# A hybrid decoder layer on one core: the recurrence's last unit, the attention's first operands and the sample's recurrence change places

## The chip, the cores and the metric

The kernel runs on one core of one Trainium2 chip. The time is that of one launch on the device, in microseconds (us); before the change it is 3038.96 us, the median of three runs (3030.53 to 3044.77). Everything lives in one program: matmuls on TensorE (PE), elementwise work on VectorE (DVE), ScalarE (ACT) and GpSimd (POOL), and nearly all transfers are issued by SyncE (SP).

## What is computed

One layer of a decoder, in float32, for a prompt of 2048 tokens and for 8 sample requests of 4 tokens each (32 rows), which share the weights:

```
a = rmsnorm(h); [qa|fa|ia|ga|qb|kb|vb] = a @ w_in          # 1024 -> 4*512 + 3*512
h = h + concat(HGRN2(qa,fa,ia,ga), DilatedAttn(qb,kb,vb)) @ w_o
h = h + ConvFFN(rmsnorm(h))                                # 1024 -> 2816 -> 1024
h = h + sigmoid(rmsnorm(h) @ w_ple_gate) * (p @ w_ple_proj)
y = rmsnorm(h)
```

HGRN2 is a gated linear recurrence with 4 heads of width 128, `S_t = diag(f_t) S_{t-1} + k_t v_t^T`, `o_t = S_t^T q_t`, which the kernel evaluates by chunks of 128 tokens. The attention has 8 heads of width 64 and three dilated windows (1, 4 and 16 apart). For the sample, both start from a given state: a matrix per request and head, and 2048 cached keys and values per request. Outputs are the two `y`, the states, the keys and values, and the shifted caches.

## The kernel before

A product of two float32 matrices is made of three fast ones: each operand is split into a rounded part and a remainder (`wh`/`wl`, `xh`/`xl`), and three of the four products are summed (`mm3`, lines 142 to 144; lines 344 to 346 when the tokens stand in the rows).

**Projections** (`in_phase`, once per block of tokens: 0 to 1023, then 1024 to 2079). Feature groups (qa, fa, ga) go to `ha_d` in DRAM, token groups to `va_d` (the recurrence's values), `v_d`, `qT_d` and `kT_d`. The second block's order is i, qa, fa, ga, a marker `H`, then v, q, k.

**The prompt's recurrence** (`hgrn_unit`): 8 units, each of 512 tokens and two heads, unit 0 first. A unit is a chain over DVE, PE, ACT and POOL in about ten steps; the state `S` of each head passes from unit to unit. The generator `hgrn(lo, hi)` makes units `lo` to `hi - 1`. Units 0 to 6 are woven into the second block's projections: 0 to 3 at two steps per group ahead of the marker, 4 to 6 at one step per group behind it. Unit 7 is woven into the attention, with the spare PSUM pool `pps` (tiles `s`).

**Attention** (`attn_phase`, stepped as `main`). For each pair of heads p and each 512 tokens c, `stage` loads rotated queries and keys from DRAM, and `stack` splits them (POOL lines 148, 654, 659; DVE 655; ACT 658). Then come units of work over 128 queries: scores on PE (762, 763), mask, add and minimum in one DVE instruction (767, it needs the constant `mask`, line 671), exponential on ACT (768), transposes (775), a copy (777) and the weighted sum (787). A head in one unit is one exponential, so the 256 exponentials count the stage's progress. Results of two dilations are merged through small DRAM round trips. The first stage's first chunk uses the tiles `ssq` and `rb` of the projections as staging.

**Beside the attention** runs the generator `others()`: unit 7 of the recurrence, then the sample's attention (`attn_sample`, 32 loads `skt` of 1 MB each from the caches, matmuls 887 and 923), then the sample's recurrence (`hgrn_sample`, lines 551 to 629: loads of the state, DVE 616, PE 610 and 613). It advances one step on every second turn of `main`.

**Trunk** (`trunk`): output projection, feed-forward (Strassen products, lines 1207 to 1360, weights prepared on ACT 180 and DVE 181, sums into `h` at DVE 1248) and embedding. `embed_prep` splits the input of the embedding (ACT 1390, DVE 1392) and sums squares for its norm (`sum_sq`: ACT 1004, add at line 1005, on POOL by `eng=G`).

**What sets the order.** The program is written as generators that are stepped against each other; a list scheduler then fixes the order of each engine's instructions when the program is built. `first(gen, n)` gives a generator's steps a priority of 1000 instructions ahead (`AHEAD`). On the chip each engine takes its own list strictly in order and waits on semaphores. SyncE's list is one queue too: a load behind a store waits until the store's data is computed. Each of its transfers also waits until the transfer eight places ahead of it has landed, since it takes that one's semaphore. Pools of SBUF are opened and closed as stacks from the left or the right; a tile in a reused place waits for the last reader of what lay there.

Of the kernel before, what the change touches and what calls it, by code (L numbers as in the profile page):

```python
# [11 lines left out]
F32 = mybir.dt.float32  # L12
# [35 lines left out]
def hymba_step_kernel(ctx: ExitStack, tc: tile.TileContext, I: dict, O: dict):  # L48
# [387 lines left out]
    def hgrn_unit(u, heads, S, ld, wk, sp, plv, po, pms, msk):  # L436

        u0 = 512 * u
        st = {}
# [80 lines left out]
        for i, h in enumerate(heads):  # L520
# [5 lines left out]
            for c in range(4):  # L526
# [3 lines left out]
                s = sp.tile([128, 128], F32, name=f"S{h}")  # L530
# [21 lines left out]
    def hgrn_sample(hp, pps):  # L552
# [50 lines left out]
        for bb in range(8):  # L603
            s0 = hp.tile([128, 4, 128], F32, name="hs0", bufs=2)
# [30 lines left out]
    def attn_phase(spare, rest):  # L635

        def stage(p, c, tiles=()):

            out = []
            for i, src in enumerate((qT_d, kT_d)):  # L640
                t = tiles[i] if tiles else dp.tile([128, 2, 512], F32, name="stage", bufs=4)
# [19 lines left out]
        first = stage(0, 0, [t[:, :1024].rearrange("p (h t) -> p h t", h=2) for t in spare])  # L661
        yield
        dp, rp, wk, sm, pS, pA, pT = rest()
# [5 lines left out]
        kL = rp.tile([128, 2, 4, 512], F32R, name="kL")  # L669
        mask = wk.tile([128, 768], F32, name="mask", bufs=1)  # L670
        SP.dma_start(mask, I["amask"])
        stack(0, *first)
        yield
# [127 lines left out]
        todo, staged = {}, []  # L801
# [9 lines left out]
        for p in range(4):  # L811
            for c in range(4):
# [6 lines left out]
                elif c:  # L819
                    at(x - 12, lambda c=c: staged.append(stage(0, c)))  # L820
                    at(x - 6, lambda c=c: stack(c, *staged.pop(0)))
# [119 lines left out]
    def trunk(cst, rp, ev, sm, tw, hp, sh, wp, dw, pmm, pdn):  # L941
# [435 lines left out]
        def embed_prep(b, s):  # L1377
# [8 lines left out]
            for m in range(NK):  # L1386
# [4 lines left out]
                sum_sq(m, hm, s.ssq, T, eng=G)  # L1391
# [128 lines left out]
    pms = args[-1]  # L1520
    plv, po = pool("h_plv", 3, space=PSUM), pool("h_po", 1, space=PSUM)
# [33 lines left out]
    for h in range(4):  # L1555
        s = sp.tile([128, 128], F32, name=f"S{h}")
# [4 lines left out]
    main, rest = None, []  # L1561
    for x in in_phase(1, *args, plv, po):
        if x == "hgrn":
            first(side, 1000)
            side = hgrn(4, 7, *psum)
            main = attn_phase(args[0][2:], lambda: rest)
            step(main, 1)
        else:
            first(side, 2 if main else 1)
    first(side, 1000)  # L1570
    in_st.close()
    pool = pools(attn_st)
    pps = pool("s_ps", 1, space=PSUM)
    rest += (pool("a_d", 2), pool("a_r", 1), pool("a_w", 3), pool("a_s", 3),
             pool("a_pS", 2, space=PSUM), pool("a_pA", 2, space=PSUM), pool("a_pT", 2, space=PSUM))
    step(main, 1)

    def others():
        yield from hgrn(7, 8, from_pool(pps, "s1", "s2"), from_pool(pps, "s1"), from_pool(pps, "s2"))
        for h in range(4):  # L1580
            SP.dma_start(O["ps"][h], S[h])
        hgrn_st.close()
        with ExitStack() as st:
            pool = pools(st)
            yield from attn_sample(pool("s_c", 1), pool("s_k", 3), pool("s_w", 1), pps)
# [169 lines left out]
```

## Time and profile before

| what | value |
|---|---|
| median of 3 runs | 3038.96 us (3030.53 to 3044.77) |
| the profiled execution: own time | 3035.49 us |
| its span, first to last instruction | 3033.7 us |
| mean granted TensorE clock | 0.987 |
| projections (first matmul to the last of line 346) | 0 to 829 us |
| attention, until the output projection's first matmul | 829 to 1225 us |
| trunk | 1225 to 3034 us |

Groups of instructions are shown as line, engine, operation, tile written and read, shape and count; then busy time, the mean of one in ns, and the idle time of the engine ahead of them with what ended it. A row of stretches gives, for each engine, the busy time and the count in the stretch, then the granted clock of PE (1.00 is full speed), the share of the 16 DMA engines that was busy, and GB/s.

### The profile page before, as it was taken

The page shows a single profiled execution, that of the slowest core. Times are in us where ns is not written, and L with a number is a line of the kernel's source. Part 1 is how long each engine was busy: PE and PEld are TensorE (multiplying, and loading weights), DVE is VectorE, ACT ScalarE, POOL GpSimd, SP SyncE. Part 2 cuts the span into 40 slices and gives each one's busy share as a digit, 9 for nine tenths or more (in the row PEclk, how much of TensorE's full clock was granted, in tenths as well). Part 3 has the DMA queues.
Part 4 walks back from the last instruction along what each step waited for, and adds up shares of the span by engine and source line. Part 5 has one row for each costly group of instructions (what it writes and reads, how often), then busy time and mean ns, then how long its engine had stood idle before and what let it go on. Part 6 is the DMA issues. An engine that isn't in the chain of part 4 may idle for free.

```text
span 3033.7 us, 52104 instructions
## 1 busy us (share of the span) xinstructions
PE 2927.9 (97%) x18639; PEld 2716.8 (90%) x18639; DVE 2252.7 (74%) x4847; ACT 1310.1 (43%) x2824; POOL 736.8 (24%) x758
## 2 busy tenths in 40 slices
PE   8999999999988899999999999999999999999998
PEld 8988799988776557999999999999999999998987
DVE  7657766876588777658988888766679777777777
ACT  5332422222166665434544444544444544444443
POOL 1343222212244443102443431000001000002331
PEclk9999999999989999999999999999999999999999
DMA  5899533342338996766666568677778777787773
GB/s 184 312 338 324 175 101 102 110 130 94 111 101 230 269 271 185 250 230 220 229 213 195 190 197 297 230 249 253 242 239 312 249 236 243 242 275 280 263 253 130
DMA packets 328579, 664.08 MB, mean 219 GB/s; under 512 B 46400, under 2 KB 114112, under 8 KB 326528
## 3 DMA queue, kind: packets, MB, share of 16 engines
q1 hardware_dynamic: 291472, 472.65, 47.8%
q0 software_dynamic: 33264, 121.13, 12.5%
q10 hardware_dynamic: 3584, 66.98, 6.0%
q8 instruction: 147, 2.41, 0.3%
q14 instruction: 112, 0.92, 0.1%
HBM read 513.69 MB, written 213.92 MB: 240 GB/s over the span
## 4 chain that ended last, share of the span: by engine, by line
PE 53%; DVE 6%; issue 2%; DMA 1%; ACT 1%; POOL 0%; SPq 0%; DVEq 0%; POOLq 0%; ACTq 0%
PE mm L142 17%; PE mm L144 17%; PE mm L143 17%; DVE h L1248 1%; DVE w L181 1%; PE acc L787 1%; PE PT L775 1%; DVE w L1392 1%; DMA w<-h_d 0%; DMA out_yT_dram<-w 0%; PE mm L129 0%; PE S L762 0%; DVE h L1098 0%; PE s L923 0%; PE s L613 0%
## 5 line engine op out<-in xcount | busy, mean ns | idle before, releaser
L143 PE MATMUL mm<-w 128*128 128x348 f32 (+3 forms) x3636 | 1166.2, 321 | 3.4 <-DVE w L1392 3.2
L142 PE MATMUL mm<-w 128*128 128x348 f32 (+3 forms) x3508 | 1110.6, 323 | 21.1 <-ACT s L1190 7.7
L144 PE MATMUL mm<-w 128*128 128x348 f32 (+3 forms) x3508 | 1117.3, 321 | 2.0 <-DVE w L181 2.0
L143 PEld LDWEIGHTS mm<-w 128*128 128x128 f32 x3636 | 684.2, 188 | 6.7 <-DVE w L1392 4.5
L142 PEld LDWEIGHTS mm<-w 128*128 128x128 f32 x3508 | 656.5, 188 | 30.4 <-ACT s L1190 9.9
L144 PEld LDWEIGHTS mm<-w 128*128 128x128 f32 x3508 | 658.9, 188 | 3.2 <-DVE w L181 2.4
L181 DVE TENSOR_TENSOR w<-raw,w 128x512 fp32r<-128x512 f32 x586 | 434.1, 746 | 182.2 <-ACT w L180 175.7
L180 ACT CAST w<-raw 128x512 fp32r<-128x512 f32 x586 | 360.5, 621 | 413.3 <-PE mm L144 295.8
L1232 POOL DMA_DIRECT2D w<-wd_d x231 | 123.9, 537 | 894.8 <-PE mm L144 788.9
L1248 DVE TENSOR_TENSOR h<-h,mm 128x348 f32<-128x348 f32 (+1 forms) x504 | 247.4, 507 | 44.4 <-PE mm L144 42.8
L768 ACT ACTIVATE P<-P,st 128x256 f32<-128x256 f32 (+3 forms) x256 | 134.3, 526 | 72.2 <-DVE st L767 66.5
L1190 ACT COPY s<-mm 128x348 f32<-128x348 f32 (+1 forms) x198 | 87.9, 444 | 154.4 <-PE mm L144 154.2
L344 PE MATMUL mm<-wh,xh 128*128 128x512 f32 x352 | 141.8, 406 | 0.0
L345 PE MATMUL mm<-wl,xh 128*128 128x512 f32 x352 | 140.5, 399 | 0.3 <-DVE wl L267 0.3
L346 PE MATMUL mm<-wh,xl 128*128 128x512 f32 x352 | 140.6, 400 | 0.0
L144 PE MATMUL mm<-xh,wl 128*128 128x384 f32 (+2 forms) x384 | 125.1, 330 | 5.0 <-DVE wl L267 5.0
L142 PE MATMUL mm<-xh,wh 128*128 128x384 f32 (+2 forms) x384 | 124.5, 329 | 5.6 <-ACT xh L242 5.3
L143 PE MATMUL mm<-xl,wh 128*128 128x384 f32 (+2 forms) x384 | 125.5, 328 | 1.7 <-DVE xl L243 1.7
L767 DVE CUSTOM_DVE_ANT_0 P<-S,mask 128x256 f32<-128x256 f32 (+3 forms) x256 | 106.1, 447 | 26.9 <-PE S L763 19.3
L1005 POOL TENSOR_TENSOR w<-w 128x696 f32<-128x696 f32 (+2 forms) x42 | 75.6, 1808 | 171.1 <-ACT w L1004 162.1
L787 PE MATMUL acc<-pt,v 128*64 128x128 f32 x1136 | 102.9, 300 | 12.8 <-DVE pt L777 11.4
L267 DVE TENSOR_TENSOR wl<-wraw,wh 128x512 fp32r<-128x512 f32 x104 | 89.1, 878 | 28.3 <-POOL wh L148 23.1
(356 smaller groups left out, 5252.5 us busy)
## 6 DMA issues: line engine op xcount, KB each, us to landing
w<-wd_d POOLq DMA_DIRECT2D x231, 512.0 KB, 5.4
wd_d<-dw SPq DMA_DIRECT2D x77, 512.0 KB
out_sk_dram<-in_cache_k_dram ACTq DMA_DIRECT2D x56, 584.0 KB
out_sv_dram<-in_cache_v_dram ACTq DMA_DIRECT2D x56, 584.0 KB
raw<-in_w_gate_dram SPq DMA_DIRECT2D x110, 256.0 KB
raw<-in_w_up_dram SPq DMA_DIRECT2D x110, 256.0 KB
wraw<-in_w_in_dram SPq DMA_DIRECT2D x104, 256.0 KB
raw<-w_gate_d SPq DMA_DIRECT2D x88, 256.0 KB
```

The costliest lines, as they stand in the source:

```text
L142: PE.matmul(ps, lhsT=wh, rhs=xh, start=first, stop=False, skip_group_check=read)
L143: PE.matmul(ps, lhsT=wh, rhs=xl, start=False, stop=False, skip_group_check=read)
L144: PE.matmul(ps, lhsT=wl, rhs=xh, start=False, stop=last, skip_group_check=read)
L180: A.copy(w[:, 0], raw)
L181: V.tensor_sub(w[:, 1], raw, f32(w[:, 0]))
L344: PE.matmul(ps, lhsT=xh[k][:, js], rhs=wh, start=k == 0, stop=False)
L345: PE.matmul(ps, lhsT=xh[k][:, js], rhs=wl, start=False, stop=False)
L346: PE.matmul(ps, lhsT=xl[k][:, js], rhs=wh, start=False, stop=k == NK - 1)
L768: A.activation(pe, pe, AF.Exp, bias=mn, scale=-1.0, accum_out=st[:, bl.r, hh, 0:1])
L787: PE.matmul(acc[hs, bl.r], lhsT=vals[bl.p, bl.di, c][:, r, hs], rhs=bl.pt[hh][:, i], start=i == 0, stop=i == bl.nk - 1, tile_position=(0, ...
L1232: G.dma_start(t, wd_d[p][n - 1])
L1248: V.tensor_add(o, o, acc[m][:, :H])
```

## The change

All eight units of the prompt's recurrence are now stepped in the second block's projections: behind the marker `hgrn(4, 8)` is stepped three steps per group. When it is done, its state is stored and its SBUF (right side) and PSUM (`more_st`) are given back; the attention's operand pool (`a_r`: qS, q4, kH, kL) and staging pool (`a_d`) open there, and the stages and stacks of the first two chunks are stepped while the projections go on. `others()` now holds the sample's recurrence first, then the sample's attention, with all their pools open at once, and advances on two turns of five. The states `S` have 5 buffers, the sample's state loads 4 instead of 2. In `embed_prep` the sum of squares is added on VectorE instead of GpSimd.

```diff
-                s = sp.tile([128, 128], F32, name=f"S{h}")
+                s = sp.tile([128, 128], F32, name=f"S{h}", bufs=5)
...
-            s0 = hp.tile([128, 4, 128], F32, name="hs0", bufs=2)
+            s0 = hp.tile([128, 4, 128], F32, name="hs0", bufs=4)
...
-        def stage(p, c, tiles=()):
+        rp, dp = early
+        spare = [t[:, :1024].rearrange("p (h t) -> p h t", h=2) for t in spare]
+
+        def stage(p, c):
...
-                t = tiles[i] if tiles else dp.tile([128, 2, 512], F32, name="stage", bufs=4)
+                t = dp.tile([128, 2, 512], F32, name="stage") if c % 2 else spare[i]
...
-        first = stage(0, 0, [t[:, :1024].rearrange("p (h t) -> p h t", h=2) for t in spare])
-        yield
-        dp, rp, wk, sm, pS, pA, pT = rest()
...
+        staged = [stage(0, 0), stage(0, 1)]
+        for c in range(2):
+            stack(c, *staged.pop(0))
+            yield
+        wk, sm, pS, pA, pT = rest
         mask = wk.tile([128, 768], F32, name="mask", bufs=1)
         SP.dma_start(mask, I["amask"])
-        stack(0, *first)
-        yield
...
-                elif c:
+                elif c > 1:
...
-                sum_sq(m, hm, s.ssq, T, eng=G)
+                sum_sq(m, hm, s.ssq, T)
...
     for x in in_phase(1, *args, plv, po):
         if x == "hgrn":
             first(side, 1000)
-            side = hgrn(4, 7, *psum)
-            main = attn_phase(args[0][2:], lambda: rest)
-            step(main, 1)
-        else:
-            first(side, 2 if main else 1)
-    first(side, 1000)
+            side, late = hgrn(4, 8, *psum), True
+        elif main:
+            step(main, 1 if begun < 2 else 0)
+            begun += 1
+        elif not first(side, 3 if late else 2) and late:
+            for h in range(4):
+                SP.dma_start(O["ps"][h], S[h])
+            hgrn_st.close()
+            more_st.close()
+            pool = pools(attn_st, side="right")
+            main = attn_phase(args[0][2:], (pool("a_r", 1), pool("a_d", 2)), rest)
+            begun = step(main, 1)
...
     def others():
-        yield from hgrn(7, 8, from_pool(pps, "s1", "s2"), from_pool(pps, "s1"), from_pool(pps, "s2"))
-        for h in range(4):
-            SP.dma_start(O["ps"][h], S[h])
-        hgrn_st.close()
         with ExitStack() as st:
             pool = pools(st)
-            yield from attn_sample(pool("s_c", 1), pool("s_k", 3), pool("s_w", 1), pps)
-        with ExitStack() as st:
-            yield from hgrn_sample(pools(st)("hsp", 1), pps)
+            cp, kp, sw, hp = pool("s_c", 1), pool("s_k", 3), pool("s_w", 1), pool("hsp", 1)
+            yield from hgrn_sample(hp, pps)
+            yield from attn_sample(cp, kp, sw, pps)
...
-        if turn % 2:
+        if turn % 5 in (1, 3):
             first(side, 1)
```

What the built program makes of it shows in the engines' lists. The first place is PE at the end of the projections (`mm` with `xh_134` is the last k-step of a group; `hq,hF` and `hM,hF` belong to unit 7, `S` to the attention's scores). Before:

```order
L346 MATMUL mm<-wh,xl_142 128x512
L367 MATMUL ms<-c_ident,ev 128x128 x4
L460 MATMUL s_8759<-hq,hF 128x128 x4
L460 MATMUL s_8765<-hq,hF 128x128 x4
L367 MATMUL ms<-c_ident,ev 128x128 x4
L484 MATMUL s_8820<-hM,hF 128x3x64 x2
L484 MATMUL s_8823<-hM,hF 128x3x64 x2
L762 MATMUL S<-kH,q_8624 128x128
```

Now (line numbers from the loop over chunks on are 3 to 8 higher than before):

```order
L346 MATMUL mm<-wh,xl_142 128x512
L367 MATMUL ms<-c_ident,ev 128x128 x8
L766 MATMUL S<-kH,q_8319 128x128
...
L767 MATMUL S<-kL,q_8319 128x128
L574 MATMUL s_9081<-hsq,hsF 32x32 x4
L574 MATMUL s_9146<-hsE,hsF 32x32 x4
...
L613 MATMUL s_9377<-hsvm,hskt 128x128 x4
```

Unit 7's matmuls have left this place, and the sample's recurrence (`hsF`, `hskt`) stands behind the scores of the first two units.

The second place is SyncE's list at the same point. Before (`stage` and `v` are loads of the attention, `kT_d` and `out_pk` stores of the projections):

```order
L643 DMA stage<-kT_d 64x2x512
L643 DMA stage<-qT_d 64x2x512
L373 DMA kT_d<-oT 512x1x128
L643 DMA stage<-qT_d 64x2x512
L643 DMA stage<-kT_d 64x2x512 x2
L671 DMA mask<-in_amask_dram 128x768
L681 DMA v<-v_d 128x4x128 x4
```

Now:

```order
L605 DMA hs_9562<-in_state_dram 128x4x128
...
L889 DMA skt<-in_kT_w_dram 128x4x512 x3
L373 DMA kT_d<-oT 512x1x128
L380 DMA out_pk_dram<-ev 128x512
L373 DMA kT_d<-oT 512x1x128
L618 DMA out_ss_dram<-hsn 128x4x128
L605 DMA hs_9641<-in_state_dram 128x4x128
L618 DMA out_ss_dram<-hsn 128x4x128
L605 DMA hs_9717<-in_state_dram 128x4x128
L677 DMA mask<-in_amask_dram 128x768
L685 DMA v<-v_d 128x4x128 x3
```

The attention's mask now stands behind three cache loads and behind the stores of the first two new sample states.

The third place is DVE at the seam from feed-forward to embedding (`c_gains` rows are the split of `embed_prep`, `h<-h,mm` the last sums of the feed-forward). Before:

```order
L1392 SCALAR_TENSOR_TENSOR w<-w,c_gains 128x696
L1248 TENSOR_TENSOR h<-h,mm 128x344
L1392 SCALAR_TENSOR_TENSOR w<-w,c_gains 128x696 x5
L1248 TENSOR_TENSOR h<-h,mm 128x344 x3
L1392 SCALAR_TENSOR_TENSOR w<-w,c_gains 128x696
```

Now:

```order
L1396 SCALAR_TENSOR_TENSOR w<-w,c_gains 128x696
L1252 TENSOR_TENSOR h<-h,mm 128x344
L1396 SCALAR_TENSOR_TENSOR w<-w,c_gains 128x696
L1009 TENSOR_TENSOR w<-w 128x696
L1396 SCALAR_TENSOR_TENSOR w<-w,c_gains 128x696
L1009 TENSOR_TENSOR w<-w 128x696
L1396 SCALAR_TENSOR_TENSOR w<-w,c_gains 128x696 x2
L1009 TENSOR_TENSOR w<-w 128x696
L1396 SCALAR_TENSOR_TENSOR w<-w,c_gains 128x696
L1252 TENSOR_TENSOR h<-h,mm 128x344 x2
```

The adds of the squares (`L1009`) have come from POOL into DVE's list, between the splits.

More of the change, by code (lines that the diff above doesn't have):

```diff
@@ L630, in hgrn_sample, with attn_phase @@
         yield
-    def attn_phase(spare, rest):
-        def stage(p, c, tiles=()):
+    def attn_phase(spare, early, rest):
+        rp, dp = early
+        spare = [t[:, :1024].rearrange("p (h t) -> p h t", h=2) for t in spare]
+        def stage(p, c):
             out = []
             for i, src in enumerate((qT_d, kT_d)):
-                t = tiles[i] if tiles else dp.tile([128, 2, 512], F32, name="stage", bufs=4)
+                t = dp.tile([128, 2, 512], F32, name="stage") if c % 2 else spare[i]
                 for half in range(2):
@@ L800, in attn_phase @@
         n = len(units)
-        todo, staged = {}, []
+        todo = {}
         def at(x, f):
@@ L1520, in hymba_step_kernel @@
     pms = args[-1]
+    more_st = ExitStack()
+    pool = pools(more_st)
     plv, po = pool("h_plv", 3, space=PSUM), pool("h_po", 1, space=PSUM)
@@ L1555, in hymba_step_kernel @@
     for h in range(4):
-        s = sp.tile([128, 128], F32, name=f"S{h}")
+        s = sp.tile([128, 128], F32, name=f"S{h}", bufs=5)
         G.memset(s, 0.0)
@@ L1560, in hymba_step_kernel @@
     side = begin()
-    main, rest = None, []
+    main, rest, late = None, [], False
     for x in in_phase(1, *args, plv, po):
@@ L1564, in hymba_step_kernel @@
             first(side, 1000)
-            side = hgrn(4, 7, *psum)
-            main = attn_phase(args[0][2:], lambda: rest)
-            step(main, 1)
-        else:
-            first(side, 2 if main else 1)
-    first(side, 1000)
+            side, late = hgrn(4, 8, *psum), True
[10 more added lines that the diff above has]
+            begun = step(main, 1)
     in_st.close()
+    pps = pools(attn_st)("s_ps", 1, space=PSUM)
+    pool = pools(attn_st, side="right")
+    rest += pool("a_w", 3), pool("a_s", 3)
     pool = pools(attn_st)
[L1573 to L1576, printed above, removed]
+    rest += [pool(n, 2, space=PSUM) for n in ("a_pS", "a_pA", "a_pT")]
     def others():
-        yield from hgrn(7, 8, from_pool(pps, "s1", "s2"), from_pool(pps, "s1"), from_pool(pps, "s2"))
-        for h in range(4):
-            SP.dma_start(O["ps"][h], S[h])
-        hgrn_st.close()
         with ExitStack() as st:
             pool = pools(st)
-            yield from attn_sample(pool("s_c", 1), pool("s_k", 3), pool("s_w", 1), pps)
-        with ExitStack() as st:
-            yield from hgrn_sample(pools(st)("hsp", 1), pps)
+            cp, kp, sw, hp = pool("s_c", 1), pool("s_k", 3), pool("s_w", 1), pool("hsp", 1)
+            yield from hgrn_sample(hp, pps)
+            yield from attn_sample(cp, kp, sw, pps)
     side = others()
```

## The prediction

> **What bounds the kernel now.** I read the page first, then a table of stretches cut at the seams between stages.
>
> ```profile
> span 3033.7 us, 52104 instructions
> PE 2927.9 (97%) x18639; PEld 2716.8 (90%) x18639; DVE 2252.7 (74%) x4847; ACT 1310.1 (43%) x2824; POOL 736.8 (24%) x758
> ...
> GB/s 184 312 338 324 175 101 102 110 130 94 111 101 230 269 271 185 250 230 220 229 213 195 190 197 297 230 249 253 242 239 312 249 236 243 242 275 280 263 253 130
> ```
>
> ```profile
> core 0: us, PE busy (x) PEld busy (x) DVE busy (x) ACT busy (x) POOL busy (x), PEclk, DMA share, GB/s
> ...
> 620.00:785.00 165.00, 163.40 (x928) 134.05 (x926) 111.98 (x327) 40.69 (x114) 41.78 (x49) 1.00 0.33 105
> 785.00:829.00 44.00, 43.65 (x221) 32.20 (x220) 16.19 (x48) 5.42 (x8) 0.00 (x0) 1.00 0.42 131
> 829.00:848.00 19.00, 11.37 (x54) 9.52 (x52) 16.86 (x31) 9.67 (x12) 16.94 (x16) 0.78 0.84 235
> 848.00:898.00 50.00, 45.86 (x338) 37.92 (x339) 42.93 (x132) 29.96 (x83) 14.86 (x13) 0.84 0.30 71
> 898.00:945.00 47.00, 38.12 (x298) 30.15 (x297) 43.49 (x136) 34.89 (x111) 31.06 (x26) 0.86 0.48 122
> 945.00:1147.00 202.00, 182.00 (x1582) 118.61 (x1584) 145.88 (x477) 126.72 (x373) 78.05 (x66) 0.96 0.95 274
> 1147.00:1225.00 78.00, 70.45 (x657) 52.91 (x649) 63.46 (x219) 42.47 (x125) 26.10 (x26) 0.96 0.63 179
> 1225.00:2740.00 1515.00, 1501.83 (x9434) 1493.96 (x9434) 1163.56 (x2029) 689.87 (x1342) 267.52 (x318) 1.00 0.72 240
> 2740.00:2770.00 30.00, 24.89 (x150) 23.11 (x151) 30.00 (x45) 12.46 (x18) 15.74 (x12) 1.00 0.53 176
> ...
> 2890.00:2960.00 70.00, 62.85 (x367) 60.32 (x365) 52.26 (x88) 35.05 (x57) 24.70 (x13) 0.97 0.68 238
> ```
>
> In the projections (620 to 829) and in the trunk up to 2740, PE is busy 99% at full clock: work added there costs its full time, work that other engines do there is free. In the attention (829 to 1225) PE is busy 348 of 396 us, at a clock of 0.78 to 0.96, and no engine is full: it goes by the chain from scores to weighted sum, with DVE at 79% on average and at 91% and 93% in two stretches. From 945 to 1147, where the caches are read, the DMA engines are busy 95%. At 2740 to 2770 DVE is full and PE idles 5 us.
>
> **Unit 7 moves into the projections: +20.** These are the recurrence's PE groups for units 0 to 6, at full clock:
>
> ```profile
> L484 PE MATMUL lv<-hM,hF 128*128 128x192 f32 x336 | 66.9, 328 | 2.1 <-DVE at L496 1.4 <-DVE D L427 0.7
> L528 PE MATMUL o<-hv,at 128*128 128x128 f32 x112 | 21.8, 276 | 0.0
> L529 PE MATMUL o<-S,hE 128*128 128x128 f32 x112 | 21.7, 275 | 0.0
> L525 PE MATMUL ms<-hv,kt 128*128 128x128 f32 x112 | 15.6, 275 | 0.0
> L460 PE MATMUL lv<-hq,hF 128*128 128x128 f32 x112 | 15.3, 275 | 0.0
> L504 PE MATMUL lv<-hE,hF 128*64 128x64 f32 x112 | 9.7, 228 | 0.0
> L515 PE MATMUL ms<-c_ident,hF 128*128 128x128 f32 x56 | 8.4, 273 | 0.3 <-DVE hF L423 0.3
> L547 PE MATMUL ms<-c_ident,at 128*128 128x128 f32 x56 | 7.6, 274 | 1.6 <-DVE at L544 1.6
> ```
>
> They sum to 167 us, 23.9 a unit. Each group's span holds the pipeline behind its last start, some 0.27 us, which the next projection matmul covers; with about 25 groups a unit that leaves 17. So 17 to 24, and 26 with stalls like the 2.1 and 1.6 above; I take 20. The projections then end at 849 instead of 829. DVE has room for the unit's some 30 us: 128 of 209 us are used from 620 on. The stacking of the first pair's four chunks goes there too, on POOL, ACT and DVE, and is hidden.
>
> **The attention's start: +4.** Now, the last projection matmul and the first exponential:
>
> ```profile
> 829.01 0.39 PE L346 MATMUL mm<-wh,xl 128*128 128x512 f32 x1
> ...
> L768 ACT ACTIVATE P<-P,st x256: 385/504/725, 848.3 to 1214.8; 128x256 f32<-128x256 f32 x76, 128x128 f32<-128x128 f32 x20, 128x384 f32<-128x384 f32 x16, 128x512 f32<-128x512 f32 x16
> ```
>
> From 829.0 to 848.3 the attention waits 19 us, for stacks, mask and unit 7 ahead on DVE. The stacks and unit 7 leave, but the mask now stands in SyncE's list behind four sample states, the constants of the sample's attention, three cache loads, three stores and two states out and in. Counted with the mask: 1.05 + 0.8 + 3.15 + 0.8 + 1.05 + 0.4 = 7.2 MB. At 274 GB/s (the row at 945) they take 26 us, at 338 (the page's best slice) 21, starting about 3 us ahead of the last matmul, since the first wait only for a middle step of the last group. The mask lands 18 to 23 us after it: I take a wait of 23, that is +4. Below, the wait could be 12, since only the sample's own chain needs time if the transfers overlap better (-7); above, see the slow rival (+15).
>
> **The first heads without unit 7: -12.** From 848 to 898 there are 65 rows of line 768, two per head: 32 heads. DVE spent there, on unit 7 (this view reaches to 905, where the unit ends):
>
> ```profile
> 848.00:898.00 50.00, 19.89 (x65) 0.84 0.30 71
> ```
>
> ```profile
> L496 DVE COPY_PREDICATED at<-msk,s 128x128 f32<-128x128 uint8 x23 | 6.5, 298 | 0.2 <-PE s L484 0.2
> L423 DVE TENSOR_TENSOR hE<-hE,D 128x256 f32<-128x256 f32 x7 | 5.7, 815 | 0.0
> L423 DVE TENSOR_TENSOR hF<-hF,D 128x256 f32<-128x256 f32 x10 | 5.5, 554 | 1.6 <-PE s L484 1.6
> ```
>
> That is 17.7 us of its 42.9, and PE spent on the unit what is left of the 20 above after the first 19 us, some 12 of 45.9. Five state updates of the sample come in, 5 x 4 x 0.34 = 7 us. By DVE 11 us are saved, by PE 12 less 5; with the stretch's fill of 92%, and the staging of chunks 2 and 3 gone, I take 12, with bounds of 6 and 20.
>
> **The sample's recurrence leaves the tail: -12.** Its main groups, and the chain from its first load to its first new state:
>
> ```profile
> L613 PE MATMUL s<-hsvm,hskt 32*128 32x128 f32 x64 | 9.2, 283 | 0.0
> L616 DVE SCALAR_TENSOR_TENSOR hsn<-hs,hsD,s 128x128 f32<-128x128 f32 x32 | 9.0, 342 | 6.5 <-PE s L613 6.5
> ```
>
> ```profile
> 1154.34 0.42 SPq L556 DMA_DIRECT2D msksf<-in_lvl_mask_s_dram  x1
> ...
> 1180.50 1.12 DVE L616 SCALAR_TENSOR_TENSOR hsn<-hs,hsD,s 128x128 f32<-128x128 f32 x4 [1.94 <-PE s L613]
> ```
>
> With the small groups about 13 us of PE and 14 of DVE leave the last 78 us, where PE is 90% busy: 4 to 16, I take 12. In the new place it runs in the 23 us of waiting, paid already.
>
> **The cache loads: +2.** From 945 to 1147 at 274 GB/s 55 MB moved, 33.6 of them the 32 loads. Now three loads land in the start's wait, and PE's list spreads the other 29 (30.4 MB) over heads 26 to 146, with some 19 MB of the attention's own: 49 MB, 180 us at that rate. The 224 heads from 898 on took 317 us, so 120 take 170. Between 0 and +12; I take 2, since PE waited for these loads so little before:
>
> ```profile
> PE s L887 <- DMA skt<-in_kT_w_dram: 5.8, 3, 4.9
> ```
>
> **The sums of squares: -4.** At the seam to the embedding:
>
> ```profile
> L1005 POOL TENSOR_TENSOR w<-w 128x696 f32<-128x696 f32 x7 | 13.5, 1925 | 0.3
> ...
> L1392 DVE SCALAR_TENSOR_TENSOR w<-w,c_gains 128x696 fp32r<-128x696 f32 x8 | 14.6, 1866 | 0.0
> ...
> L1024 DVE TENSOR_TENSOR w<-w 128x696 fp32r<-128x696 f32 x2 | 3.4, 1682 | 0.0
> ...
> 2739.66 0.93 DVE L1392 SCALAR_TENSOR_TENSOR w<-w,c_gains 128x696 fp32r<-128x696 f32 x1
> ...
> L1005 DVE TENSOR_TENSOR w<-w x28: 424/880/885, 1253.2 to 3021.4; 128x696 f32<-128x696 f32 x14, 128x688 f32<-128x688 f32 x7, 128x256 f32<-128x256 f32 x7
> ```
>
> The split takes 0.93 us ahead of the POOL adds and 1.87 on average beside them. Eight splits lose 7.2 us less, seven adds cost 7 x 0.88 = 6.2 more, and two subtractions that ran long beside them (line 1024, 1.68 where an add takes 0.88) save 1.6: -2.7 where DVE is full. For the third block (2890 to 2960, PE idle 7 us) another -1; the second is under full PE. Bounds: -9, if all of those 7 come back, and +1, if the adds bring no relief. [...]
>
> **Sum.** 20 + 4 - 12 - 12 + 2 - 4 = -2, against the profiled execution's 3035.5 (span 3033.7): 3033.5. The median of the runs lies 3.5 above that execution, so the forecast is 3037. A difference of this kernel is told from none at about 0.5%, 15 us.
>
> **Rivals.** (1) Slower: SyncE's list. If the sample's chain takes as long as above, 26 us to its first state and some 6 more to its second, the mask leaves 29 us after the last matmul and lands at 34: +11 over my sum. Each further store of a state then holds the loads behind it; at the old place this took
>
> ```profile
> SPq L618 <- DVE hsn L616: 13.5, 6, 4.2
> ```
>
> Together some +22: 3059. For it: the list; against: nothing competes with the chain while the attention waits. It decides from a first exponential 35 us after the last projection matmul. (2) Faster: the unit costs 17, the wait is 12, the first heads gain 20, the tail 16, the seam 6: -30, so 3009 to 3012. For it: the clock of 0.78 to 0.86 up to 945, which less waiting would lift; against: the mask's place. (3) The move stalls PE, because four units in one go and the stacks fill DVE: 112 us of DVE in 165 plus 31 is 87%. If the stacks' POOL work held DVE too, this row gives 2 x 1.62 a chunk for the keys, 13 for four, and the queries' step is of the same kind; with some 24 in all DVE would be full:
>
> ```profile
> L659 POOL TENSOR_TENSOR kL<-stage,kH 128x512 fp32r<-128x512 f32 x30 | 47.9, 1617 | 14.7 <-DMA coef_d<-wt 7.0 <-ACT kH L658 2.9 <-issue 2.2
> ```
>
> Some 12 of it would reach PE: 3049. Against it: the stacks come when the units are done, where DVE idles 28 of the 44 us from 785. [...]
>
> **Chances.** Forecast 0.50; (1) 0.18; (2) 0.27; (3) 0.05. The forecast's own range is 3024 to 3052. The range that should hold 8 in 10 reaches to (2) and to (1): 3010 to 3062. Faster by over 0.5% 0.27; within 0.51; slower 0.22.
>
> **What would show it.** The last projection matmul at 846 to 853; the first exponential 20 to 27 us later; 32 heads within 40 us from there; the cache loads' last matmul near 1080; the output projection's first matmul at 1218 to 1230; eight splits at the seam near 0.9 us each. I am wrong if the attention takes under 355 us from the last projection matmul, or over 390.

## The result, and the profile after

The changed kernel takes 3046.56 us (median of 15 runs, 3035.99 to 3058.00) against 3038.96 before. Over all runs of both the ratio is 1.0036, with a 95% interval of 1.0026 to 1.0045: 11 us slower (8 to 14). The two medians alone differ by 7.6 us. The forecast was 3037. The change is inside the 0.5% that the prediction calls no change, but the forecast missed by 10 us and on the other side of zero. Below, 0.001 of a ratio is counted as 3.04 us.

The profiled execution took 3048.89 us (span 3047.1). First the last projection matmul, the exponentials (first and last start) and the first matmul of the output projection, from the timeline and the views by line, of after:

```profile
856.50 0.39 PE L346 MATMUL mm<-wh,xl 128*128 128x512 f32 x1
L772 ACT ACTIVATE P<-P,st x256: 385/507/727, 884.1 to 1234.5; 128x256 f32<-128x256 f32 x76, 128x128 f32<-128x128 f32 x20, 128x384 f32<-128x384 f32 x16, 128x512 f32<-128x512 f32 x16
1241.74 0.59 PE L142 MATMUL mm<-w 128*128 128x348 f32 x2 [1.40 <-ACT w L1027]
```

The projections end 27.5 us later than before (829.0), the wait for the first exponential is 27.6 us in place of 19.3, and the attention from the last projection matmul to the output projection takes 385.2 us; before it was 396.2, by this row of before:

```profile
1225.23 0.94 PE L142 MATMUL mm<-w 128*128 128x348 f32 x2 [1.02 <-ACT w L1023]
```

So in these two traces the attention gave back 11 us of the 27.5 that the projections took longer. Where it did, the exponentials show (two rows a head). In the table of stretches for their line, the first row reaches to head 32, the second from there to head 224, the third from there to the last. Of after:

```profile
core 0: us, ACT busy (x), PEclk, DMA share, GB/s
884.00:933.00 49.00, 19.42 (x66) 0.86 0.70 199
...
932.80:1198.30 265.50, 108.02 (x385) 0.93 0.80 210
1198.30:1235.20 36.90, 20.83 (x66) 1.00 0.28 78
```

and of before, whose first 32 heads took 50 us by the row in the prediction:

```profile
898.10:1162.20 264.10, 107.59 (x384) 0.94 0.86 245
1162.20:1215.50 53.30, 20.34 (x64) 1.00 0.56 162
```

The tail is 16 us shorter: no work of the sample is left in it. The middle is unchanged. And the first 32 heads, which have lost unit 7, take as long as with it. The table of stretches of all engines says what took its place:

```profile
core 0: us, PE busy (x) PEld busy (x) DVE busy (x) ACT busy (x) POOL busy (x), PEclk, DMA share, GB/s
829.00:856.60 27.60, 27.60 (x131) 22.24 (x130) 12.51 (x30) 4.89 (x6) 8.85 (x8) 1.00 0.41 122
856.60:884.00 27.40, 16.87 (x138) 12.83 (x136) 12.22 (x55) 2.46 (x3) 5.60 (x9) 0.63 1.02 320
884.00:898.00 14.00, 13.52 (x67) 9.40 (x66) 6.20 (x31) 7.43 (x27) 4.39 (x4) 0.51 0.96 222
898.00:915.00 17.00, 17.00 (x137) 12.80 (x137) 13.50 (x55) 11.32 (x33) 0.00 (x0) 1.00 0.34 79
915.00:933.00 18.00, 18.00 (x143) 9.96 (x144) 9.64 (x27) 8.01 (x20) 0.00 (x0) 1.00 0.85 295
```

From 884 to 933 PE is busy 48.5 of 49 us, for 14 of them at a clock of 0.51. DVE has room: it is busy 29 of the 49. PE's groups by shape, from 884 to 898 (first fence), from 898 to 915 and from 915 to 933, name the guests:

```profile
L613 PE MATMUL s<-hsvm,hskt 32*128 32x128 f32 x16 | 4.1, 436 | 0.0
L610 PE MATMUL s<-hs,hsEb 128*32 128x128 f32 x16 | 1.3, 420 | 0.0
```

```profile
L613 PE MATMUL s<-hsvm,hskt 32*128 32x128 f32 x16 | 2.3, 283 | 0.0
```

```profile
L891 PE MATMUL s<-skt,qb 128*32 128x512 f32 x48 | 6.0, 600 | 0.0
```

Lines 613 and 610 are the sample's recurrence, line 891 the products of the first six cache loads (eight rows a load). And the wait ahead of 884 is the mask's, in SyncE's timeline:

```profile
875.34 1.02 SPq L618 DMA_DIRECT2D out_ss_dram<-hsn  x1
876.45 1.08 SPq L605 DMA_DIRECT2D hs<-in_state_dram  x1
877.58 0.68 SPq L677 DMA_DIRECT2D mask<-in_amask_dram  x1
```

It is issued 21 us after the last projection matmul, right behind a new state's store and the load of the next state.

### The profile page after: what moved, and what is told of

It is laid out like the page before. It is cut to its first block, busy times and chain, and to the rows that moved or that the text cites. A ratio compares the mean times of both kernels' runs of the same rounds, so it can differ in the third digit from the quotient of the medians.

```text
span 3047.1 us, 52118 instructions
## 1 busy us (share of the span) xinstructions
PE 2946.9 (97%) x18639; PEld 2728.8 (90%) x18639; DVE 2250.0 (74%) x4868; ACT 1309.3 (43%) x2824; POOL 697.8 (23%) x737
## 4 chain that ended last, share of the span: by engine, by line
PE 77%; DVE 8%; DMA 8%; issue 3%; POOL 1%; ACT 1%; SPq 1%; DVEq 0%; POOLq 0%; ACTq 0%
PE mm L142 19%; PE mm L143 18%; PE mm L144 18%; PE mm L344 2%; PE mm L346 2%; PE mm L345 2%; PE lv L484 2%; PE acc L791 2%; PE PT L779 1%; DVE h L1252 1%; DMA draw<-in_w_down_dram 1%; DMA cf<-coef_d 1%; PE S L766 1%; DMA wd_d<-dw 1%; DMA skt<-in_v_d_dram 1%
## 5 line engine op out<-in xcount | busy, mean ns | idle before, releaser
L181 DVE TENSOR_TENSOR w<-raw,w 128x512 fp32r<-128x512 f32 x586 | 425.0, 730 | 178.1 <-ACT w L180 171.9
L791 PEld LDWEIGHTS acc<-pt,v 128*64 128x64 f32 x1136 | 69.2, 143 | 52.5 <-issue 17.5
L181 DVE TENSOR_TENSOR dw<-draw,dw 128x512 fp32r<-128x512 f32 x77 | 67.7, 887 | 55.5 <-ACT dw L180 54.8
```

The lines of the kernel that those rows point to most:

```text
L181: V.tensor_sub(w[:, 1], raw, f32(w[:, 0]))
L791: PE.matmul(acc[hs, bl.r], lhsT=vals[bl.p, bl.di, c][:, r, hs], rhs=bl.pt[hh][:, i], start=i == 0, stop=i == bl.nk - 1, tile_position=(0, ...
```

## The experiments

My theory after this reading: unit 7 costs its full time in the projections, and the attention does not return it, because the sample's own work, which unit 7 used to keep back as the first of the side work, has come to the front in its place. Rivals: that the attention's pace returns little whatever stands at its front; that the mask's place in SyncE's list is the whole of it; that the loss comes from elsewhere (in the trace of after the recurrence's first unit starts 5 us later than in that of before).

Every ratio below is to runs of the kernel before on the same chip, with its 95% interval.

### The parts that could be taken alone

The `eng=G` of `embed_prep` alone (line 1391 of the kernel before):

```diff
-                sum_sq(m, hm, s.ssq, T, eng=G)
+                sum_sq(m, hm, s.ssq, T)
```

> The kernel before with one edit of the change alone, the sums of squares of embed_prep on VectorE. The theory (the seam to the embedding gives back what the trace after shows there, 5.4 us, and the start of the program, whose order this edit leaves as it was, keeps its 21.7 us of PE idle time): 5 us less than before, 3034. The rival (the seam's gain is an artefact of the other edits): within 1 us of before, 3039.

Measured: 0.9979 (0.9969 to 0.9989), 6.4 us less. The part holds and works by itself. Its trace has the last projection matmul at 834.6 with an unchanged list of the projections, 5.6 us later than before's 829.0: so the 5 us at the start in the trace of after are within what executions of one list differ by.

The kernel before without unit 7:

```diff
-        yield from hgrn(7, 8, from_pool(pps, "s1", "s2"), from_pool(pps, "s1"), from_pool(pps, "s2"))
+        for h in (2, 3):
+            SP.dma_start(mix_d[:, h, 1536:SEQ], ha_d[0][:, h, 1536:SEQ])
```

> The kernel before without unit 7 of the recurrence (the last 512 tokens of heads 2 and 3 are not computed; a copy of the queries' rows stands in their place, and the prompt's last states of those two heads are those of token 1535). It measures what the attention gives back when the unit is gone and nothing else moves. The theory (the attention goes by waits, its chain and the clock, so it returns about half of what the unit takes of PE): last projection matmul still at 829, 32 heads in 42 to 45 us in place of 50, the output projection's first matmul 8 to 12 us earlier, 3027 to 3031. The rival (the attention returns PE's full 20 us): 3019.

Measured: 0.9978 (0.9967 to 0.9990), 6.7 us less: the attention returns a third of the unit. The way there was not the expected one. Its first exponential came 33 us after the last projection matmul and 32 heads took 52 us, not 42 to 45: with unit 7 gone the cache loads came to the front.

The kernel after without unit 7:

```diff
-            side, late = hgrn(4, 8, *psum), True
+            side, late = hgrn(4, 7, *psum), True
...
+            for h in (2, 3):
+                SP.dma_start(mix_d[:, h, 1536:SEQ], ha_d[0][:, h, 1536:SEQ])
```

> The kernel after without unit 7 (the same rows filled by the same copy). The theory (the unit costs the projections 22 to 23 us, its PE work of 17 and stalls of 5, and nothing of the attention depends on it any more): last projection matmul at 833 to 836 in place of 856.5, the attention from there to the output projection's first matmul unchanged at 383 to 388, 3022 to 3026. The rival (the projections' slack takes up part of the unit, and the loss comes from elsewhere): last matmul at 845 or later, 3034 or more.

Measured: 0.9967 (0.9955 to 0.9980), 10.0 us less than before and 21 less than after. Its last projection matmul is at 833.9, 22.6 us earlier, as expected; the attention took 390 us, a little over the expected band. So the unit costs the projections 21 to 23 us, and the rival of a slack there falls. Unit in the projections +21, unit out of the attention -6.7, seam -6.4: these add to 8 of the 11 us measured. But the change has a fourth part, the recurrence's move, and that is worth another -7.9 by itself (next but one section): added one by one the parts come to 0, so in the change they do not add up.

### Is it the mask's place?

The mask in a pool of its own at a place that comes free earlier, and the load ahead of the sample's:

```diff
-        mask = wk.tile([128, 768], F32, name="mask", bufs=1)
-        SP.dma_start(mask, I["amask"])
+        mask = mp.tile([128, 768], F32, name="mask")
+        with tc.high_priority(2 * AHEAD):
+            SP.dma_start(mask, I["amask"])
...
+    rest += [pools(attn_st)("a_m", 1)]
```

> The kernel after with the attention's mask in a place that comes free earlier, so that its load stands ahead of all of the sample's loads in SyncE's list; the values' loads stay where they are. The theory (the mask's place in the list costs the start of the attention some 13 us, and PE's idle time there the half clock of 24 us behind it): first exponential 12 to 16 us after the last projection matmul in place of 27.6, 32 heads within 42 us in place of 49, the end 15 to 22 us earlier, 3025 to 3032. The rival (the start waits next for the values, which stand at the same place of the list as the mask did, or is paid back by the cache loads): first exponential early, but the end less than 6 us earlier, 3040 to 3046.

Measured: 1.0036 (1.0019 to 1.0053), no better than after. The first exponential came 17 us after the last projection matmul, 10 earlier, and the 32nd head at the same time as in after (932.6 against 932.9 us): from the first exponential to there PE was busy 56.4 of 58.2 us. That speaks against the theory as I had put it: the mask was a wait in front of a busy PE. Part of the miss is the edit's own cost. PE's longest wait in the last 16 us of the attention, and what was being loaded there (waits, then DMA issues of that stretch), of this run:

```profile
PE mm L142 <- ACT w L1028: 9.6, 1, 9.6
...
raw<-in_w_o_dram SPq DMA_DIRECT2D x13, 256.0 KB
```

In after, the same wait is 1.4 us and no weight of the output projection is loaded that late:

```profile
PE mm L142 <- ACT w L1027: 1.4, 1, 1.4
```

The mask now lies in memory that the first weights of the output projection reuse. They are loaded from 1234 us on in place of 1159, and PE waits 8 us longer for them. Every run with the mask moved has this wait: the output projection begins 16 to 17 us after the last exponential, in place of 7.

### Where does the sample's recurrence stand well?

The recurrence ahead of the sample's attention, in the kernel before:

```diff
-            yield from attn_sample(pool("s_c", 1), pool("s_k", 3), pool("s_w", 1), pps)
-        with ExitStack() as st:
-            yield from hgrn_sample(pools(st)("hsp", 1), pps)
+            cp, kp, sw, hp = pool("s_c", 1), pool("s_k", 3), pool("s_w", 1), pool("hsp", 1)
+            yield from hgrn_sample(hp, pps)
+            yield from attn_sample(cp, kp, sw, pps)
```

> The kernel before with the sample's recurrence ahead of the sample's attention, and nothing else moved: term D of the prediction by itself. The theory (the recurrence's PE work of some 13 us costs about the same at the front as in the tail, since PE is full in the first heads too): the tail from head 224 on shorter by 10 to 16 us, the first part longer by about as much, the end within 4 us of before, 3034 to 3042. The rival (the prediction: at the front it lies in a wait that is paid already): 12 us less, 3026.

Measured: 0.9974 (0.9964 to 0.9984), 7.9 us less; between the two, nearer the prediction. But not by the prediction's way. Behind unit 7 the recurrence's products ran from 976 to 1013 us, in the middle, and not at the front. And the tail did not get shorter. The exponentials' stretches of this run, from head 32 to head 224 and from there to the last:

```profile
895.60:1147.80 252.20, 107.20 (x385) 0.96 0.78 221
1147.80:1205.80 58.00, 20.67 (x64) 1.00 0.92 288
```

The tail took 5 us more than before's 53, since the cache products, now last in the list, ran into it up to 1199 us. The gain lay in the middle, 252 us in place of 264.

The kernel after with the mask first and these two calls in the old order again:

> The kernel after with the mask's load ahead of all of the sample's loads and, beside that, the sample's recurrence last again (behind the sample's attention, as before). The theory (the first heads are held by PE, which then has the cache products in place of the recurrence, and the tail takes the recurrence back): first exponential 12 to 18 us after the last projection matmul, 32 heads in 42 to 47 us, head 224 to 255 back to 45 to 53 us, the end at 3042 to 3050, no better than after. The rival (the recurrence at the front, with its chain and its half clock, is what the first heads lose to): 32 heads in under 40 us and the end at 3034 or less.

Measured: 1.0048 (1.0032 to 1.0064), 3051, slightly above the expected band. The first exponential came 5.5 us after the last projection matmul, earlier than expected, and 32 heads took 60 us (858.5 to 918.1), longer than either side had it: the front is now filled by the caches. The tail did not grow back (36.7 us from head 224 to the last, where after had 36.1), since the recurrence's products ran from 1071 to 1107 us, ahead of it. The output projection began 16 us after the last exponential, the price of the mask's place again. The rival, that the recurrence alone is what spoils the front, falls: other work does it as well, though less. Head 32 came 65 us after the last projection matmul, with the mask moved and the recurrence at the front it was 76, and with neither at the front, in a run below, 43.

Without the recurrence of the sample at all, in after and in before (all else of `hgrn_sample` is left out; the two copies fill its outputs):

```diff
         for h in range(4):
...
+            SP.dma_start(mix_d[:, h, SEQ:NTOK], ha_d[0][:, h, SEQ:NTOK])
         yield
         for bb in range(8):
...
+            SP.dma_start(O["ss"][bb], I["state"][bb])
```

> The kernel after without the sample's recurrence (its states are copied from in to out and its rows of the mix are filled by copies, so its PE, DVE and ACT work is gone and its bytes stay). What the recurrence costs at the front. The theory: 8 to 14 us, so 3033 to 3039. The rival (it lies in the paid wait): at most 3 us, 3044 or more.

> The kernel before without the sample's recurrence, the same copies in its place. What it costs in the tail. The theory and the prediction agree on 10 to 14 us: 3025 to 3029. If the tail hid it, 3036 or more. What decides is the difference to the run without it at the front.

Measured: 0.9955 (0.9938 to 0.9971) and 0.9959 (0.9942 to 0.9975), 13.7 and 12.5 us under before. So the recurrence costs 12.5 us at the end of before, as expected, and some 25 in after (from 10.9 above before to 13.7 under it), far above the 8 to 14 expected. But the 25 are not the front's: in the trace without the recurrence the wait is 26.5 us and the first 32 heads still take 48.8 (first row, to head 32; second, to head 224):

```profile
873.90:922.70 48.80, 19.41 (x65) 0.94 0.99 278
922.70:1170.50 247.80, 107.56 (x384) 0.95 0.71 188
```

The cache loads moved up in its place, their first product to 855 us. What got shorter is the middle, by 18 us, and in this trace the projections, which end at 847.5 in place of 856.5; why they do is not shown. The states' copies run at the program's start, so the attention is rid of the recurrence's bytes as well, and what part they have in this no run here separates.

### The sample's work held back

All loads of the sample's recurrence, and the constants and keys of the sample's attention, behind the store of the attention's fourth statistics, at about head 32, in the kernel after. The cut shows one of the loads; the others are held in the same way. The side work's turns change too: it starts at turn 31, and then has every second turn:

```diff
+    def behind(i):
+        return tc.issue_after(marks[i].ins)
...
-            SP.dma_start(s0, I["state"][bb].rearrange("h k v -> k h v"))
+            with behind(3):
+                SP.dma_start(s0, I["state"][bb].rearrange("h k v -> k h v"))
...
+                        marks.append(SP.dma_start(stats_d[p][512 * c:512 * c + 512].rearrange("(i r) c -> i r c", r=4),
...
-        if turn % 5 in (1, 3):
+        if turn > 30 and turn % 2:
             first(side, 1)
```

> The kernel after with all loads of the sample's recurrence and attention placed in SyncE's list behind the store of the statistics of the fourth block of queries (about head 32), so that neither its loads nor its PE work can come to the front. The theory (unit 7, as the first of the side work, kept the sample's work back until head 76; with the unit gone that work came to the start, where its loads stand ahead of the mask and its products on a PE that is full and partly at half clock): first exponential 10 to 17 us after the last projection matmul in place of 27.6, 32 heads in 36 to 42 us in place of 49, the attention from the last projection matmul to the output projection's first at 362 to 373 in place of 385, the end at 3022 to 3032. The rival (the attention's pace gives back 7 us for the unit whatever stands at its front): 3041 or more.

Measured: 0.9943 (0.9922 to 0.9963), 3017.07 us: 17 us faster than before and 28 faster than after, by its median the fastest kernel of this study. Its trace, by the same views as above (exponentials of the first 32 heads; all engines in that stretch; the output projection's first matmul):

```profile
L781 ACT ACTIVATE P<-P,st x256: 384/504/725, 867.5 to 1203.9; 128x256 f32<-128x256 f32 x76, 128x128 f32<-128x128 f32 x20, 128x384 f32<-128x384 f32 x16, 128x512 f32<-128x512 f32 x16
867.40:899.80 32.40, 18.88 (x66) 0.90 0.37 72
```

```profile
867.40:899.80 32.40, 31.86 (x264) 25.34 (x264) 22.89 (x78) 25.95 (x76) 3.05 (x2) 0.90 0.37 72
899.80:1211.00 311.20, 284.25 (x2494) 196.49 (x2492) 246.12 (x810) 200.03 (x588) 135.41 (x116) 0.96 0.88 239
```

```profile
1211.32 0.61 PE L142 MATMUL mm<-w 128*128 128x348 f32 x2 [1.40 <-ACT w L1041]
```

The last projection matmul is at 856.3. The wait is 11 us, 32 heads take 32 us, the attention 355. PE is full in the first 32 heads even with the attention alone (31.86 of 32.40), and has 27 us to spare in the rest. There the sample's work went: from head 32 to the output projection it takes 311 us, and after took 309 with the recurrence and the products of six cache loads done already.

The same hold in the kernel before without unit 7:

> The kernel before without unit 7, and with the sample's loads behind the same store. The theory: now the attention gives back the 16 to 22 us of the unit instead of 7, so 3016 to 3022. The rival: 3029 to 3033, as without the hold.

Measured: 0.9949 (0.9934 to 0.9964), 15.5 us under before, where it had been 6.7 without the hold. The attention does return the unit once nothing else takes its place. The rival of a pace that returns a third of it falls.

The two parts of the change that move no unit, together in the kernel before:

> The kernel before with two parts of the change alone: the sample's recurrence ahead of its attention and the sums of squares on VectorE; unit 7 and the stacks stay where they were. If the parts add up, 8 and 6 us less than before: 3022 to 3026. If they share a gain: 3028 or more.

Measured: 0.9951 (0.9933 to 0.9968), 15 us less: the two add up (7.9 + 6.4). This is as good as the held kernel within the intervals, with unit 7 left in the attention.

The kernel after with the hold much later:

> The kernel after with the sample's recurrence held to the sixth and its caches to the eighth store of statistics (heads 80 and 96), so that both stand about where the kernel before with the recurrence first has them. The theory: the same start as the run with the hold at head 32, and a middle in which loads and heads overlap as well: 3018 to 3030. If the caches come too late and hold the end: the last cache product at the last head or behind it, and 5 us or more above that run.

Measured: 0.9976 (0.9964 to 0.9989), 7 us under before. The first 32 heads took 32 us here too, and the last cache product came at 1188 us, 15 ahead of the last exponential, so the caches did not hold the end. But the output projection began 13 us after the last exponential, where the held kernel needs 7. The first weights of the output projection were issued at 1196 us, against 1161 in the held kernel, and PE waited 9.6 us for them, as in the runs with the mask moved, though the mask had its old place.

### Loads or products?

Both remedies at once, mask first and hold:

> The kernel after with both: the mask's load first, and the sample's loads behind head 32's store. If the start waits for the mask still (5.1 us of waiting for it in the run with the hold alone), first exponential 5 to 8 us after the last projection matmul in place of 11.2 and the end 2 to 6 us below that run: 3011 to 3015. If the next wait (stacks, the clock) takes its place: within 2 us of it, 3015 to 3019.

Measured: 0.9961 (0.9947 to 0.9976), not below the hold alone. The first exponential came 5 us after the last projection matmul, as expected, in place of 11. Two things took that back. The first 32 heads took 40.5 us in place of 32, so that head 32 came 45 us after the last projection matmul, where the hold alone had 43; over the first 20.5 of these us the clock was 0.67 and PE was busy for 17.6. And the output projection began 17 us after the last exponential in place of 7, by the mask's new place.

The mask first and the sample's loads at the front, but its matmuls behind the last matmul of the fourth block's weighted sums in PE's list (`marks[3]` is that matmul here):

```diff
-        if turn % 5 in (1, 3):
-            first(side, 1)
+        if turn > 30 and turn % 2:
+            with tc.issue_after(marks[3].ins):
+                first(side, 1)
-    first(side, 1000)
+    with tc.issue_after(marks[3].ins):
+        first(side, 1000)
```

> The kernel after with the mask's load first (as in the run of the mask alone), the sample's loads left at the front, but all of the sample's matmuls behind the weighted sums of the fourth block (about head 32) in PE's list. Seven loads of 0.26 and 1.05 MB still stand ahead of the values. The theory that PE's work at the front is what the first heads lose to: first exponential 8 to 17 us after the last projection matmul, 32 heads in 32 to 40 us, the end at 3016 to 3026. The rival (the loads are, by holding the values and filling the DMA engines): 32 heads in 44 us or more, the end at 3035 or more.

Measured: 0.9990 (0.9979 to 1.0002), 14 us below the run with the mask alone, so the products, with the stores and loads that hang on them, do cost at the front. The end, 3032, lay between the two expectations. But 32 heads took 46 us, as the rival had it, because the loads held the values. The stretch in which PE stood, and its wait:

```profile
870.00:880.00 10.00, 0.49 (x6) 0.49 (x8) 0.00 (x0) 0.02 (x1) 0.00 (x0) 0.66 1.11 305
...
PE acc L794 <- DMA v<-v_d: 9.7, 1, 9.7
```

With the mask ahead of the sample's loads, the values behind them become the wait. The same without moving the mask, so that the seam stays as it was:

> The kernel after with the sample's matmuls alone held in PE's list behind the weighted sums of the fourth block (about head 32). Its first loads keep their places ahead of the mask (5.4 MB in place of 7.2, since no new state can be stored before its product), and the mask keeps its place in memory, so nothing changes for the loads of the output projection. With the kernel after (both at the front) and the run with the loads held (neither at the front) it splits the loss. If the products are the larger part: 32 heads in 31 to 38 us, first exponential 17 to 26 us after the last projection matmul, the end at 3022 to 3031, so that the products cost 15 us or more and the loads 5 to 14. If the loads are: 3035 to 3045.

Measured: 1.0005 (0.9989 to 1.0021). In its trace the last projection matmul is at 852.8, the first exponential at 876.9 and the 32nd head at 910.4:

```profile
876.80:910.40 33.60, 19.29 (x65) 0.92 0.35 70
1223.34 0.95 PE L142 MATMUL mm<-w 128*128 128x348 f32 x2 [1.40 <-ACT w L1031]
...
DVE P L773 <- DMA mask<-in_amask_dram: 16.1, 1, 16.1
```

Wait and heads came as expected for the products, the end as expected for the loads. The attention takes 385.2 us with loads and products at the front, 370.6 with the loads alone, 355.0 with neither: 15 us for each in these executions. By the medians it is 9 us for the products and 19 for the loads, with intervals of some 6 to 8 us to either side. Both count; which is larger is not settled.

## Why the prediction was wrong

**Unit 7 into the projections, +20: right, a little small.** Without and with the unit the runs differ by 21 us. The last projection matmul lies at 852 to 857 us in the eight traces that have the unit there and no copies at the program's start, and at 827 to 835 in the six that keep the projections of before. The row from 829.0 to 856.6 shows why: PE 27.60 of 27.60 at full clock.

**The attention's start, +4: the right mechanism, under-sized.** The wait grew by 8.3. The mask was issued 21 us after the last matmul, and the first exponential followed at 27.6; the forecast had 23, rival (1) 35. The forecast made the 7.2 MB a matter of bandwidth alone. SyncE's waits between 850 and 884 show two that stand between the last matmul and the mask, for the new states that are stored and for the buffers of the states that are loaded:

```profile
SPq L618 <- DVE hsn L616: 3.3, 2, 3.0
SPq L605 <- PE s L613: 2.9, 3, 1.1
```

That is rival (1)'s mechanism, smaller than it had it. What it is worth, the last run shows best: with the products held and the first loads left, no state's store stands ahead of the mask, which is issued 11.5 us after the last matmul, and the wait is still 24.1. So some 3.5 us are the stores and buffers (with 1.8 MB less ahead of the mask, too), and the rest is the loads' own time, as the forecast had it with 23. With the sample's loads held, the wait is 11 us.

**The first heads, -12: the step that failed most.** Measured: -1. The terms taken away were right: with a free front 32 heads take 32 us, 18 less than before. What failed is what was put in their place: "Five state updates of the sample come in", 7 us of DVE. The order at hand showed more: state products up to head 17, and the first cache products from head 26 on. PE's price for them is 4.1 + 1.3 us in the stretch from 884, 2.3 for the next rows of line 613 and 6.0 us for the caches: 14 us in all, as much as the unit's own rows take of PE from 848 to 898 in before (14; the prediction had 12). And PE was priced by the 92% of the stretch before, as if the rest were room. Of the 4 us that PE idled there, 3 were the weighted sums waiting for DVE, which was busy 19.6 of the 22 us from 848 to 870 (PE's groups by shape in that stretch, of before):

```profile
L787 PE MATMUL acc<-pt,v 128*64 128x128 f32 x32 | 4.2, 395 | 3.1 <-DVE pt L777 3.1
```

That idle time left with the unit. With PE busy 48.5 of the 49 us, every guest cost its whole time, and at the low clock more: sixteen rows of line 613 took 4.1 us at 0.51 and the next sixteen 2.3 at full clock. The low clock is no news of the change, though: before had 0.66 over the 22 us from 848.

**The sample's recurrence out of the tail, -12: the tail got shorter, but not by this move, and its new place was not free.** From head 224 on 16 us were saved, and taking the recurrence away from the kernel before saves 12.5. But the move alone, with unit 7 still in front, left the tail 5 us longer, because the cache products took its place there. And with unit 7 gone the tail is short with the recurrence last, too: 40.1 us in the kernel before without the unit, 36.7 in after with the old order of the two calls. So what emptied the tail is that all side work started earlier, not the recurrence's place in it; that the size came out is luck. "In the new place it runs in the 23 us of waiting, paid already" counted a place that was free only until 884: half of the state products ran behind that, in the heads that were to gain. The terms for the first heads and for the recurrence spent the same idle PE time twice. Alone, the move is worth 7.9 us, and by its trace these lie in the middle.

**The cache loads, +2, and the sums of squares, -4: right.** Heads 32 to 224 took 1.4 us longer. The sums of squares alone gave 6.4; the seam shows the eight splits beside VectorE's own adds (VectorE's groups around that seam, of after):

```profile
L1396 DVE SCALAR_TENSOR_TENSOR w<-w,c_gains 128x696 fp32r<-128x696 f32 x8 | 7.4, 941 | 0.0
L1009 DVE TENSOR_TENSOR w<-w 128x696 f32<-128x696 f32 x7 | 6.2, 879 | 0.0
```

0.94 us each in place of 1.87 beside POOL, 7.4 us less in all, against 6.2 for the adds. Measured alone the term is -6.4 with an interval of -3.3 to -9.4, in which the forecast's -4 lies.

**The rivals.** (1) named the cause of the longer wait, but priced it at 3059 by a stall that did not come. (3) fell: from 620 us to the last projection matmul PE idled 2.2 us, against 2.0 before. No run shows the 24 us or so for which it had POOL's work on the stacks hold DVE: in the trace of after single instructions of DVE ran long beside that work (a cast of line 658 took 1.70 us at 832.6, where the line's median is 0.64), but DVE was busy 32.6 of the 44 us from 785. That its 3049 lies nearest to the measured time is luck. (2) had its large gain in the first heads, which came only with the front kept free; the clock that less waiting was to lift was 0.84 over these heads in before, 0.86 in after with a longer wait, and 0.90 with the front free and a wait of 11 us. None of them was that the front of the attention fills up with other work, and none looked at PE there.

**The sum.** With the sizes of the two traces in its own terms, 27.5 + 8.3 - 1.1 for the first three (some 5 of the 27.5 are the later start of that execution), and from head 32 to the output projection 1.4 - 16.4 - 3.1 (the last from the last exponential on), the trace stands 16.5 us behind at the output projection and 13.4 at the end. The 3 us between are the seam, less what differs in the trunk.

**What stays open.** The held kernel is 17 us faster than before. Unit into the projections +21, out of the attention -15.5, the recurrence moved -7.9 and the sums -6.4 make -9. Each of these has an interval of 3 to 5 us to either side, some 8 for the sum, and the held kernel's own is -24 to -11, so the two are not told apart. If the difference is real, its cause is open: the parts were measured in kernels whose cache loads stand elsewhere. Nor has any run shown that moving unit 7 is worth anything by itself: the kernel before with the other two parts alone is as fast.

## What to carry to other kernels

When a piece of work is taken out of a list, ask what it kept back. The next entry moves up, with its loads, into the place that was to become shorter; here it took what unit 7's leaving should have given, and holding its loads back, with its turns started later, turned a loss of 11 us into a gain of 17. In the same way a piece taken from the end of a list shortens the end only if nothing slides into its place: the recurrence's move alone left the tail 5 us longer.
Price a guest by the engine that is full once the gap's owner has gone, not by the idle share seen while it was there; and do not let two terms use the same idle time.

## What the runs showed of the hardware

The clock of PE stayed low in stretches in which PE was busy. From 884 to 898 of after it was 0.51 with PE busy 13.52 of 14.00 us, and in the kernel after without unit 7 it was 0.50 for 22 us, with PE busy 21.46 of them:

```profile
863.00:885.00 22.00, 21.46 (x101) 15.62 (x102) 11.22 (x53) 11.57 (x39) 4.38 (x4) 0.50 0.76 183
```

What the granted clock goes by, these rows do not show. A matmul row of the recurrence took 436 ns at the clock of 0.51 and 283 at full clock by the rows of line 613, so in after not only the wait of 27.6 us was lost, but also time in the 14 us of slower heads behind it.

SyncE held loads back for landings that they do not read. In the trace of before four loads of the attention's values waited 9.0 us in all for cache loads, each eight places ahead of the load that waited:

```profile
SPq L684 <- DMA skt<-in_v_w_dram: 9.0, 4, 3.3
```
